# Loading and splitting an MLP's first six weight factors inside the product before it

## The chip, the cores and the metric

The kernel runs on one core of a Trainium2 chip. A core has a matrix engine (TensorE, PE in the profile; its weight loads are shown as PEld), a vector engine (VectorE, DVE), a scalar engine (ScalarE, ACT), a general engine (GpSimd, POOL) and SyncE (SP), which here only issues DMA transfers. Each engine works through its own queue in order and waits on semaphores for the others. The metric is the device time of one execution in microseconds, the median of several executions.

## The reference, cut to what matters

Two layers, each a mixer and a squared-ReLU MLP. The first layer's mixer is an mLSTM, the second's a short gated convolution. Both end in a product with an output matrix of 1024 x 1024, and an MLP follows each.

```python
D_MODEL = 1024; SEQ = 512; DEPTH = 2; D_FF = 4 * D_MODEL

def rms_norm(x, g):
    y = x * lax.rsqrt(jnp.mean(x * x, axis=-1, keepdims=True) + EPS)
    return y * g

def sqrelu_mlp(x, w_up, w_down):
    h = jax.nn.relu(x @ w_up)
    return (h * h) @ w_down

def reference(...):
    for i in range(DEPTH):
        g = norm_g[i]
        h = rms_norm(x, g[0])
        h = mlstm_mixer(h, ...) if i == 0 else short_conv_mixer(h, ...)   # ends: ... @ w_out
        x = x + rms_norm(h, g[1])
        h = sqrelu_mlp(rms_norm(x, g[2]), w_mlp_up[i], w_mlp_down[i])
        x = x + rms_norm(h, g[3])
    return x
```

All is float32.

## The kernel before

**Precision.** Every float32 operand of a product is split into a high factor, which is the operand rounded to the matrix engine's faster format, and a low factor, the rest. `split` (lines 80-85) does it in two instructions: a cast on ScalarE (line 81) and a subtraction on VectorE (line 82). `mm3` (lines 113-118) then issues three matmuls for one product: high by high, high by low, low by high.

**Buffers.** Tiles come from rings of fixed size. The ring `u` has 15 places (`NU`) of 8 KB per partition; a split weight piece or factor takes one, and so does each part of the transposed activations. The ring `raw` has 7 places (`NRAW`) for weights as they land from memory. The ring `t2` has 8 places (`NT2`) of 2 KB for intermediate values. In PSUM, where matmuls write, there are 4 banks `pu`, 2 banks `pd` and 2 banks `pt`.

**The order of instructions.** The code emits instructions in a program order. A planner of the framework, which runs when the program is built, sets the order in each engine's queue from that order and from when it takes each instruction and its buffer to be ready. A ready instruction can so be put ahead of an earlier one that waits. Beside that the code holds a queue of its own: `put_off(us, fn)` (line 141) stores a function, and `step(us)` (line 144), called along the products with their estimated microseconds, calls it when the time is up. It puts off the transposes of a token tile (`turn`, line 274) by `LATE` = 10.4.

**The output product.** `last_product` (lines 297-363) multiplies 4 token tiles of 128 tokens (t = 0 to 3) by a 1024 x 1024 matrix in two halves of 512 columns. Its 8 weight pieces (4 for each half) are loaded and split and stay in 8 places of `u` until the last token tile has used them. The order on PE is: half 0 of t=0 and t=1, half 1 of t=0 and t=1, then both halves of t=2, then both of t=3. `done` (line 320) takes each result out of its `pd` bank with a square-and-sum on ScalarE (line 198) and a multiplication on VectorE (line 332). After the second half of a token tile, `tail` adds the normed row to the residual (line 291), norms it again (line 269) and puts its transposes off (line 278, PE). `Seven.take` (line 228) then splits the transposed tile into the parts that the MLP needs. For t=0 and t=1 these are the parts `a11` and `a12`. For t=2 and t=3 they are `p1`, `r3`, `p4`, `n2` and `a22`, sums and differences of all four blocks. With t=0 it also takes two places of `raw` (`keep`).

**The MLP.** The up product of `mlp` (lines 899-965) is computed in 8 column groups (`quad(g)`, 512 columns each) by a scheme of seven block products in place of eight (class `Quad`, lines 818-894). One block product (`prod`, line 805) is 24 matmuls with a moving size of 256. `begin` (line 842) loads the weight block (0,0), splits it, multiplies it by `a11` and copies the result to a `t2` tile (line 847). `first_done` (line 849) does the same with block (1,0) and `a12`, adding in the same PSUM bank. These two need only token tiles 0 and 1. `run` (line 854) does the other five products, which need `p1`, `r3`, `p4`, `n2` and `a22` and so all token tiles. For the first 3 groups (`AHEAD`), `begin` and `first_done` stand at the head of `mlp`, before any `run`, so that PE has work while the last token tiles are being normed. Then the groups alternate with the down product (`down`, line 921), and `last_product` ends the MLP too, without a mixer after it.

Program order around the change, twice in the kernel (line 803 with line 968, line 1007 with line 1008): the whole of `last_product`, then `mlp` with 3 x `begin`, 3 x `first_done`, `flush()`, `run` of groups 0 and 1, `down(0)` and so on.

Of the kernel before, what the change touches and what calls it, by code (L numbers as in the profile page):

```python
# [36 lines left out]
AHEAD = 3  # L37
# [3 lines left out]
def tile_hybrid_trunk(  # L41
# [29 lines left out]
    def pd():  # L71
        return psum("pd", 2)
# [40 lines left out]
    def mm3(o, lhs, rhs, first, last):  # L113
        lh, ll = lhs
        rh, rl = rhs
        nc.tensor.matmul(o, lh, rh, start=first, stop=False, skip_group_check=True)  # L116
        nc.tensor.matmul(o, lh, rl, start=False, stop=False, skip_group_check=True)  # L117
        nc.tensor.matmul(o, ll, rh, start=False, stop=last, skip_group_check=True)  # L118


    def rows_of(hT, k, t):
        c = (t % 2) * P
        return [hT[k // 2][:, i, t // 2, k % 2, c : c + P] for i in range(2)]
# [20 lines left out]
    def step(us):  # L144
        for item in queue:
            item[0] -= us
        while queue and queue[0][0] <= 0:
            queue.pop(0)[1]()

    def flush(n=0):  # L150
        while len(queue) > n:
            queue.pop(0)[1]()
# [22 lines left out]
    def gain(i, k):  # L175
        g = const.tile([P, D], F32, tag="gain", name="gain", bufs=2)
        nc.gpsimd.dma_start(g, norm_g[i, k].partition_broadcast(P))
        return g
# [79 lines left out]
    def halves(n=2):  # L258
        return [slice(i * D // n, (i + 1) * D // n) for i in range(n)]
# [34 lines left out]
            if store is not None:  # L294
                nc.sync.dma_start(store[:, hs], xt[:, hs])

    def last_product(wm, r0, hT, g, tail, accs=None, ends=False):

        flush()
        ws = {}  # L300
        parts = [halves() for _ in range(NT)]
        if ends:
            parts[NT - 1] = halves()[:1] + halves(4)[2:]
        ygs = [[] for _ in range(NT)]
        mss = [None] * NT

        def ks(o, t, cs, k0, k1):
            hf, c0 = divmod(cs.start, 512)
            n = cs.stop - cs.start
            for k in range(k0, k1):  # L310
                w = ws[hf][k // 2]
                mm3(
                    o[:, 0:n],
                    rows_of(hT, k, t),
                    (w[:, 0, k % 2, c0 : c0 + n], w[:, 1, k % 2, c0 : c0 + n]),
                    k == 0,
                    k == KO - 1,
                )

        def done(o, t, cs):  # L320
            n = cs.stop - cs.start
            step(BLOCK * n / 512)
            i = len(ygs[t])
            if i == 0:
                mss[t] = small(len(parts[t]))
            yg = half_kb(n=n)
            ygs[t].append((cs, yg))
            last = i == len(parts[t]) - 1
            o = o[:, 0:n]
            if accs is None:  # L330
                part_ms(o, mss[t], i)
                nc.vector.tensor_tensor(out=yg, in0=o, in1=g[:, cs], op=ALU.mult)  # L332
            else:
                y = accs[t][:, cs]
                nc.vector.tensor_tensor(out=y, in0=y, in1=o, op=ALU.add)  # L335
                part_ms(y, mss[t], i)
                eng = nc.vector if ends and t == NT - 1 else nc.gpsimd
                eng.tensor_tensor(out=yg, in0=y, in1=g[:, cs], op=ALU.mult)
            if last:
                tail(t, ygs[t], mss[t])  # L340

        for hf in range(2):
            ws[hf] = [
                piece(
                    wm[r0 + 2 * i * P : r0 + 2 * (i + 1) * P, halves()[hf]].rearrange(
                        "(k p) m -> p k m", p=P
                    ),
                    2,
                )
                for i in range(4)  # L350
            ]
            os = [pd() for _ in range(2)]
            first = KO - 2 if hf == 0 else 0
            for t in range(2):
                ks(os[t], t, parts[t][hf], 0, first)
            for t in range(2):
                ks(os[t], t, parts[t][hf], first, KO)
                done(os[t], t, parts[t][hf])
        for t in range(2, NT):
            for cs in parts[t]:  # L360
                o = pd()
                ks(o, t, cs, 0, KO)
                done(o, t, cs)
# [3 lines left out]
    xT = Plain()  # L367
# [174 lines left out]
    a = T1[0:H, :]  # L542
# [203 lines left out]
    hT = [None] * (KO // 2)  # L746
# [41 lines left out]
    def tail_to(gn, nxt, aside=False):  # L788
        def tail(t, yg, ms2):
            if nxt is None:  # L790
                add_normed(yg, ms2, xs[t], out2[t * P : (t + 1) * P, :])
            else:
                add_normed(yg, ms2, xs[t], None)
                pre_norm(t, xs[t], gn, nxt, LATE)
                if aside:
                    nc.gpsimd.dma_start(xd[t], xs[t])

        return tail
# [1 line left out]
    for t in range(NT):  # L800
        load_x(t)
    xT2 = Seven()
    last_product(w_out_mlstm[0], 0, hT, gain(0, 1), tail_to(gain(0, 2), xT2, True))

    def prod(o, fw, fx, first):

# [11 lines left out]
    class Quad:  # L818
# [20 lines left out]
        def values(self):  # L839
            return by_tile(half_kb())  # L840

        def begin(self, a=None):
            f = self.factor(a if a is not None else self.block(0, 0))
            self.x = pu()
            prod(self.x, f, self.xT.f["a11"], True)
            self.s1 = self.values()
            nc.scalar.copy(self.s1, by_tile(self.x))

        def first_done(self, c=None):
            f = self.factor(c if c is not None else self.block(1, 0))  # L850
            prod(self.x, f, self.xT.f["a12"], False)
            self.take(0, 0, self.values(), by_tile(self.x))

# [42 lines left out]
    def by_tile(o):  # L896
        return o.rearrange("p (u n) -> p u n", u=2)

    def mlp(i, xT, gy, tail, ends=False):
        NG = FF // P // G  # L900
        hs = [None] * (FF // P // 2)

        def quad(g):
            def take(nh, half, c, o):
                j = 2 * g + nh
                if o is not None:
                    nc.scalar.activation(c, o, AF.Relu)
                else:
                    o = c
                nc.vector.scalar_tensor_tensor(  # L910
                    out=c, in0=o, scalar=0.0, in1=c, op0=ALU.max, op1=ALU.mult
                )
                if hs[j] is None:
                    hs[j] = pair()
                split(hs[j][:, 0, half], hs[j][:, 1, half], c)

            return Quad(w_up[i], g * 512, g * 512 + 256, xT, take)

        ys = []

        def down(g):
            if g == 0:
                ys.extend(token_tiles())
            for hf, cs in enumerate(halves()):
                ws = [
                    piece(
                        w_dn[i][r * P : (r + 2) * P, cs].rearrange("(k p) m -> p k m", p=P), 2
                    )
                    for r in (g * G, g * G + 2)
                ]  # L930
                for t in range(NT):
                    o = pd()
                    for k in range(G):
                        w = ws[k // 2]
                        mm3(
                            o,
                            rows_of(hs, g * G + k, t),
                            (w[:, 0, k % 2, :], w[:, 1, k % 2, :]),
                            k == 0,
                            k == G - 1,  # L940
                        )
                    yh = ys[t][:, cs]
                    if g == 0:
                        nc.scalar.copy(yh, o)
                    else:
                        nc.vector.tensor_tensor(out=yh, in0=yh, in1=o, op=ALU.add)  # L946


        flush(2)
        quads = [quad(g) for g in range(NG)]  # L950
        for qd in quads[:AHEAD]:
            qd.begin()
        for qd in quads[:AHEAD]:
            qd.first_done()
        flush()
        for g in range(2):
            quads[g].run(True)
        for g in range(NG - 2):
            down(g)
            quads[g + 2].run(g + 2 < AHEAD)  # L960
            if g == NG - 4:
                xs[:] = token_tiles()
                for t in range(NT):
                    nc.gpsimd.dma_start(xs[t], xd[t])  # L964
        last_product(w_dn[i], FF - D, hs[-(KO // 2) :], gy, tail, ys, ends)

    xT3 = Plain()
    mlp(0, xT2, gain(0, 3), tail_to(gain(1, 0), xT3))


    us = {}
    yT = [None] * (KO // 2)
# [31 lines left out]
        [(w_in_conv[0], seg[i % 3] + (i // 3) * P) for i in range(3 * KO)], xT3, take_c, 6  # L1004
    )
    xT4 = Seven()
    last_product(w_out_conv[0], 0, yT, gain(1, 1), tail_to(gain(1, 2), xT4, True))
    mlp(1, xT4, gain(1, 3), tail_to(None, None), ends=True)


# [29 lines left out]
```

## Time and profile before

| | us |
|---|---|
| three runs: median (lowest to highest) | 1138.42 (1138.06 to 1138.58) |
| the profiled execution | 1139.16 |
| its span, from the first to the last instruction | 1137.4 |
| PE busy in the span | 1098.1 |
| DVE busy | 733.9 |
| ACT busy | 450.2 |

The profile shows one execution with start and duration of each instruction, and for each idle stretch of an engine the instruction that ended it ("<-"). Times in its rows are microseconds from the start of the span. A row of grouped instructions gives the line of the code, the engine, the operation, the output and input tiles, the shape and the count. The times of matmul ends are modelled, and a few per cent of matmul records can be missing. The granted clock (PEclk) is the share of full speed that TensorE had in a stretch of time.

### The profile page before, as it was taken

The numbers are of one execution on the slowest core, as the hardware profiler recorded it, in microseconds if no ns is written. First come the engines' busy times: TensorE is split into PE (matmuls) and PEld (weight loads), VectorE is DVE, ScalarE is ACT, GpSimd is POOL, SyncE is SP. The second block draws the span as 40 slices with busy tenths as digits, with TensorE's granted clock in tenths as the row PEclk, the third lists the DMA queues.
The fourth block names the chain that finished last, engine by engine and source line by source line (L and its number), as shares of the span: only waits on it lengthen the run. The fifth ranks groups of instructions, "written<-read, shape, count | busy, mean of one in ns | idle before, by whom it ended". The sixth has DMA issues, their size and how long they took to land.

```text
span 1137.4 us, 15341 instructions
## 1 busy us (share of the span) xinstructions
PE 1098.1 (97%) x6243; PEld 949.2 (83%) x6243; DVE 733.9 (65%) x993; ACT 450.2 (40%) x692; POOL 64.9 (6%) x108
## 2 busy tenths in 40 slices
PE   8999999969999999999999999996999999999997
PEld 5878887869798898899889888786978889889986
DVE  5552665469776776767685444346977677676763
ACT  6431543346444244234363222234644424423421
POOL 2000100110000000000130000011000000000011
PEclk9999999989999999999999999998999999999999
DMA  8420363044353243153535331104435324315301
GB/s 263 135 67 1 101 214 93 38 158 157 117 162 96 71 130 104 64 186 103 138 88 172 113 106 59 56 37 145 151 119 160 94 74 130 104 64 185 103 28 56
DMA packets 112749, 126.35 MB, mean 111 GB/s; under 512 B 4998, under 2 KB 85158, under 8 KB 112679
## 3 DMA queue, kind: packets, MB, share of 16 engines
q1 hardware_dynamic: 109366, 113.31, 32.0%
q0 software_dynamic: 3312, 12.06, 2.9%
q8 instruction: 49, 0.80, 0.3%
q14 instruction: 22, 0.17, 0.1%
HBM read 119.07 MB, written 6.29 MB: 110 GB/s over the span
## 4 chain that ended last, share of the span: by engine, by line
PE 73%; DVE 11%; issue 9%; ACT 3%; DMA 2%; POOL 1%; SPq 0%; POOLq 0%; DVEq 0%; ACTq 0%
PE pu L116 12%; PE pu L117 12%; PE pu L118 12%; PE pd L117 11%; PE pd L118 11%; PE pd L116 11%; DVE u L82 4%; DMA raw<-in_w_in_mlstm_dram 1%; ACT u L81 1%; ACT junk L198 1%; DMA raw<-in_w_mlp_up_dram 1%; DVE t L910 1%; POOL small L190 1%; DVE u L291 1%; DVE hb L82 1%
## 5 line engine op out<-in xcount | busy, mean ns | idle before, releaser
L116 PE MATMUL pu<-u 128*128 128x256 f32 (+1 forms) x1296 | 408.2, 315 | 19.1 <-ACT u L81 18.8
L118 PE MATMUL pu<-u 128*128 128x256 f32 (+1 forms) x1296 | 403.2, 312 | 4.4 <-DVE u L82 4.4
L117 PE MATMUL pu<-u 128*128 128x256 f32 (+1 forms) x1296 | 404.8, 312 | 0.4 <-DVE u L82 0.4
L82 DVE TENSOR_TENSOR u<-raw,u 128x1024 fp32r<-128x1024 f32 (+1 forms) x248 | 295.4, 1204 | 137.7 <-ACT u L81 137.4
L81 ACT CAST u<-raw 128x1024 fp32r<-128x1024 f32 (+1 forms) x248 | 251.4, 1035 | 272.0 <-PE pd L118 118.3
L116 PEld LDWEIGHTS pu<-u 128*128 128x128 f32 x1296 | 246.0, 190 | 36.5 <-ACT u L81 20.5
L118 PEld LDWEIGHTS pu<-u 128*128 128x128 f32 x1296 | 245.1, 189 | 20.7 <-DVE u L82 6.0
L117 PEld LDWEIGHTS pu<-u 128*128 128x128 f32 x1296 | 246.0, 190 | 16.3 <-DVE u L82 1.3
L117 PE MATMUL pd<-u,hb 128*128 128x512 f32 (+1 forms) x648 | 254.2, 392 | 1.3 <-DVE u L82 1.3
L116 PE MATMUL pd<-u,hb 128*128 128x512 f32 (+1 forms) x648 | 254.5, 393 | 0.7 <-ACT u L81 0.4
L118 PE MATMUL pd<-u,hb 128*128 128x512 f32 (+1 forms) x648 | 253.9, 392 | 0.0
L117 PEld LDWEIGHTS pd<-u,hb 128*128 128x128 f32 x648 | 121.7, 188 | 30.1 <-DVE u L82 2.9
L116 PEld LDWEIGHTS pd<-u,hb 128*128 128x128 f32 x648 | 121.5, 188 | 29.3 <-DVE t L332 1.2
L118 PEld LDWEIGHTS pd<-u,hb 128*128 128x128 f32 x648 | 121.7, 188 | 28.1
L81 ACT CAST hb<-t 128x512 fp32r<-128x512 f32 x80 | 49.1, 621 | 86.1 <-DVE t L910 74.2
L946 DVE TENSOR_TENSOR u<-u,pd 128x512 f32<-128x512 f32 x80 | 54.7, 683 | 29.6 <-PE pd L118 29.5
L198 ACT ACTIVATE junk<-u 128x512 bf16<-128x512 f32 (+1 forms) x49 | 30.5, 623 | 77.7 <-DVE u L335 48.3
L82 DVE TENSOR_TENSOR hb<-t,hb 128x512 fp32r<-128x512 f32 x80 | 53.4, 687 | 3.8 <-ACT hb L81 3.6
L332 DVE TENSOR_TENSOR t<-pd,gain 128x512 f32<-128x512 f32 x16 | 11.0, 688 | 36.3 <-ACT junk L198 36.3
L964 POOL DMA_DIRECT2D u<-xd x8 | 4.3, 536 | 493.6 <-PE pu L118 493.6
L910 DVE SCALAR_TENSOR_TENSOR t<-t 128x512 f32<-128x512 f32 x48 | 31.5, 685 | 0.0
L291 DVE SCALAR_TENSOR_TENSOR u<-t,small,u 128x512 f32<-128x512 f32 (+1 forms) x33 | 22.9, 733 | 10.8 <-POOL small L190 10.8
(153 smaller groups left out, 664.8 us busy)
## 6 DMA issues: line engine op xcount, KB each, us to landing
raw<-in_w_mlp_up_dram SPq DMA_DIRECT2D x76, 512.0 KB, 3.7
raw<-in_w_mlp_down_dram SPq DMA_DIRECT2D x64, 512.0 KB, 3.5
raw<-in_w_in_mlstm_dram SPq DMA_DIRECT2D x24, 512.0 KB, 4.8
raw<-in_w_in_conv_dram SPq DMA_DIRECT2D x24, 512.0 KB, 5.3
raw<-in_w_out_mlstm_dram SPq DMA_DIRECT2D x8, 512.0 KB, 4.1
xd<-u POOLq DMA_DIRECT2D x8, 512.0 KB, 2.9
u<-xd POOLq DMA_DIRECT2D x8, 512.0 KB, 5.8
raw<-in_w_out_conv_dram SPq DMA_DIRECT2D x8, 512.0 KB, 3.5
```

Source lines behind the costliest of these rows:

```text
L81: hi = nc.scalar.copy(dst_hi, src)
L82: lo = nc.vector.tensor_tensor(out=dst_lo, in0=src, in1=dst_hi.bitcast(F32), op=ALU.subtract)
L116: nc.tensor.matmul(o, lh, rh, start=first, stop=False, skip_group_check=True)
L117: nc.tensor.matmul(o, lh, rl, start=False, stop=False, skip_group_check=True)
L118: nc.tensor.matmul(o, ll, rh, start=False, stop=last, skip_group_check=True)
L190: nc.gpsimd.tensor_tensor(out=r, in0=r, in1=mhalf[:, 0:1], op=ALU.pow)
L198: nc.scalar.activation(junk(n), src, AF.Square, scale=float(D) ** -0.5, accum_out=ms[:, i : i + 1])
L291: nc.vector.scalar_tensor_tensor(out=xt[:, hs], in0=y, scalar=r, in1=xt[:, hs], op0=ALU.mult, op1=ALU.add)
L332: nc.vector.tensor_tensor(out=yg, in0=o, in1=g[:, cs], op=ALU.mult)
L910: nc.vector.scalar_tensor_tensor(out=c, in0=o, scalar=0.0, in1=c, op0=ALU.max, op1=ALU.mult)
L946: nc.vector.tensor_tensor(out=yh, in0=yh, in1=o, op=ALU.add)
L964: nc.gpsimd.dma_start(xs[t], xd[t])
```

## The change

`mlp` becomes a generator in three parts. The first part makes the eight `Quad` objects and calls a new `prepare` on the first three: load block (0,0) and split it. The second part calls `prepare_more` on them: load block (1,0) and split it. The third part is the rest, with `begin` and `first_done` using the prepared factors. `last_product` takes a function `ahead` and calls it at the head of the token tiles t=2 and t=3, so that the first part is emitted between t=1 and t=2, and the second between t=2 and t=3. The gains that `mlp` needs are made by functions called in its third part. Both MLPs are treated alike. No instruction is added or removed; the order of the program changes.

```diff
-    def last_product(wm, r0, hT, g, tail, accs=None, ends=False):
+    def last_product(wm, r0, hT, g, tail, accs=None, ends=False, ahead=None):
...
         for t in range(2, NT):
+            if ahead is not None:
+                ahead()
             for cs in parts[t]:
                 o = pd()
                 ks(o, t, cs, 0, KO)
...
-    last_product(w_out_mlstm[0], 0, hT, gain(0, 1), tail_to(gain(0, 2), xT2, True))
...
+        def prepare(self):
+            self.f1 = self.factor(self.block(0, 0))
+
+        def prepare_more(self):
+            self.f2 = self.factor(self.block(1, 0))
+
         def begin(self, a=None):
-            f = self.factor(a if a is not None else self.block(0, 0))
+            f = self.factor(a) if a is not None else self.f1
             self.x = pu()
             prod(self.x, f, self.xT.f["a11"], True)
...
         def first_done(self, c=None):
-            f = self.factor(c if c is not None else self.block(1, 0))
+            f = self.factor(c) if c is not None else self.f2
             prod(self.x, f, self.xT.f["a12"], False)
...
-    def mlp(i, xT, gy, tail, ends=False):
+    def mlp(i, xT, gain_of, tail_of, ends=False):
...
+        quads = [quad(g) for g in range(NG)]
+        for qd in quads[:AHEAD]:
+            qd.prepare()
+        yield
+        for qd in quads[:AHEAD]:
+            qd.prepare_more()
+        yield
+        gy, tail = gain_of(), tail_of()
 
         flush(2)
-        quads = [quad(g) for g in range(NG)]
         for qd in quads[:AHEAD]:
             qd.begin()
...
-    mlp(0, xT2, gain(0, 3), tail_to(gain(1, 0), xT3))
+    m = mlp(0, xT2, lambda: gain(0, 3), lambda: tail_to(gain(1, 0), xT3))
+    last_product(
+        w_out_mlstm[0], 0, hT, gain(0, 1), tail_to(gain(0, 2), xT2, True), ahead=lambda: next(m)
+    )
+    for _ in m:
+        pass
...
-    last_product(w_out_conv[0], 0, yT, gain(1, 1), tail_to(gain(1, 2), xT4, True))
-    mlp(1, xT4, gain(1, 3), tail_to(None, None), ends=True)
+    m = mlp(1, xT4, lambda: gain(1, 3), lambda: tail_to(None, None), ends=True)
+    last_product(
+        w_out_conv[0], 0, yT, gain(1, 1), tail_to(gain(1, 2), xT4, True), ahead=lambda: next(m)
+    )
+    for _ in m:
+        pass
```

## The prediction, made before the changed kernel ran

> **What bounds the kernel now.** I read the page's engine totals first, then the costliest groups, then the waits, then the timeline of each engine around the longest PE wait.
>
> ```profile
> span 1137.4 us, 15341 instructions
> PE 1098.1 (97%) x6243; PEld 949.2 (83%) x6243; DVE 733.9 (65%) x993; ACT 450.2 (40%) x692; POOL 64.9 (6%) x108
> ...
> L116 PE MATMUL pu<-u 128*128 128x256 f32 (+1 forms) x1296 | 408.2, 315 | 19.1 <-ACT u L81 18.8
> ```
>
> PE is busy for 1098.1 of 1137.4 us, so 39.3 us of idle time are all that a new order can win besides the clock. Of these, 18.8 us stand before one group, waiting for the cast of a split (line 81). The timeline of PE has them in two places, one for each mixer's output product with the MLP behind it:
>
> ```profile
> 233.79 1.04 PE L278 MATMUL pt<-ident,t 128*128 128x128 f32 x8
> ...
> 243.97 0.58 PE L116 MATMUL pu<-u 128*128 128x256 f32 x1 [9.14 <-ACT u L81]
> ...
> 774.11 1.03 PE L278 MATMUL pt<-ident,t 128*128 128x128 f32 x8
> ...
> 784.29 0.58 PE L116 MATMUL pu<-u 128*128 128x256 f32 x1 [9.15 <-ACT u L81]
> ```
>
> PE ends the transposes of t=2 at 234.8 (775.1) and starts `begin` 9.1 us later. The ScalarE timeline shows why:
>
> ```profile
> 234.86 0.59 ACT L247 COPY t<-pt 128x512 f32<-128x512 f32 x1
> ...
> 237.05 1.14 ACT L81 CAST u<-t 128x512 fp32r<-128x512 f32 x2
> 240.70 0.63 ACT L198 ACTIVATE junk<-u 128x512 bf16<-128x512 f32 x1 [2.51 <-DVE u L291]
> ...
> 241.32 1.12 ACT L81 CAST u<-raw 128x512 fp32r<-128x512 f32 x2
> 242.35 0.61 ACT L81 CAST u<-t 128x512 fp32r<-128x512 f32 x1
> 242.87 4.84 ACT L81 CAST u<-raw 128x1024 fp32r<-128x1024 f32 x5
> ```
>
> The weights' casts (128x1024) come right behind the five casts of t=2's parts (`p1` and `r3` at 237.05, `p4` and `n2` at 241.32, `a22` at 242.35). The input of `a22` was copied at 234.86, and ScalarE idled for 2.51 us before 240.70, yet `a22` waited for `p4` and `n2`. I read this as places of the ring `u` being given out in program order: `a22` and the six factors stand behind `p4`, and `p4` behind the chain on VectorE. The weights were not late:
>
> ```profile
> 185.57 1.50 SPq L828 DMA_DIRECT2D raw<-in_w_mlp_up_dram  x2
> ...
> SPq L828 <- DVE u L82: 92.6, 15, 59.2
> ```
>
> The last two loads before the gap are issued by 187, and the next waits 59.2 us for a place of `raw` that only a split frees.
>
> **What follows the gap** decides how much of it is won. The windows (busy time, instructions, then granted clock, DMA share and GB/s):
>
> ```profile
> 190.00:234.00 44.00, 43.81 (x198) 35.32 (x197) 16.13 (x29) 13.43 (x34) 5.08 (x9) 1.00 0.10 40
> ...
> 244.00:250.00 6.00, 6.00 (x38) 5.74 (x39) 6.00 (x7) 4.12 (x5) 0.58 (x1) 0.74 0.47 132
> 250.00:256.00 6.00, 6.00 (x54) 6.00 (x53) 3.28 (x3) 1.70 (x3) 0.00 (x0) 1.00 1.09 360
> 264.00:300.00 36.00, 32.90 (x252) 30.53 (x250) 33.73 (x44) 16.04 (x22) 0.00 (x0) 1.00 0.47 147
> ...
> 784.00:790.00 6.00, 5.71 (x26) 5.45 (x27) 6.00 (x8) 4.03 (x5) 0.00 (x0) 0.52 0.32 96
> 790.00:796.00 6.00, 6.00 (x53) 6.00 (x52) 3.64 (x4) 2.27 (x4) 0.00 (x0) 1.00 1.02 320
> 804.00:840.00 36.00, 33.58 (x263) 31.85 (x262) 33.73 (x45) 16.09 (x22) 0.00 (x0) 1.00 0.45 144
> ```
>
> Three things are to be seen. In the output product (190 to 234) PE is full while VectorE and ScalarE have 28 and 30 us free. Behind the gap the clock is low for some us: 38 matmuls in 6 us against 54 in the next 6, which is 6 x 16/54 = 1.8 us lost; in the second place 26 against 53, less 0.3 idle, up to 2.7. And from 264 to 300 VectorE is the fuller engine (33.73 of 36 against 32.90), with PE idle for 3.1 us (2.4 in the second place). So the gain goes through two engines, and the later one decides.
>
> **The change part by part.** Moved are 2 x 6 loads, casts and subtractions; none is added or removed. Their price:
>
> ```profile
> L82 DVE TENSOR_TENSOR u<-raw,u 128x1024 fp32r<-128x1024 f32 x240 | 290.1, 1221 | 137.0 <-ACT u L81 136.7
> ...
> L81 ACT CAST u<-raw 128x1024 fp32r<-128x1024 f32 x240 | 246.7, 1049 | 269.4 <-PE pd L118 118.3 <-PE pu L118 71.6 <-DVE raw L860 32.7
> ```
>
> *Where they go.* By count of `u`: at t=2 eight weight pieces and two token tiles hold 10 of 15 places. The first three factors make 13, `a11` and `a12` make 15. The second three need places that the pieces of half 0 free when t=3's half 0 ends (about 228), and one that the old token tiles free earlier. Then 2 + 6 + 1 token tile + 4 pieces make 13, and with t=3 done the five parts make 14: all fit. Three casts are 3.1 us, three subtractions 3.7 us, in an output product with 28 us free: I cost them at nothing. If that cover is gone, an eviction waits, which is a rival below. The loads are earlier on SP's queue, where the output product's own pieces are already through, and the later loads (blocks of `run`) get their `raw` places about 10 us earlier.
>
> *PE.* The gap of 9.1 goes and the cold clock with it: 10.9 us (11.9 in the second place). Three `begin` products take 3 x 24 matmuls, at 54 in 6 us 8.0 us, so PE is at 242.8 and wants `first_done`, which must wait until the copy of `begin`'s result (line 847) has left the bank.
>
> ```profile
> L847 ACT COPY t<-pu 128x512 f32<-128x512 f32 x16 | 9.4, 586 | 23.2 <-PE pu L118 23.2
> ...
> 243.77 1.41 DVE L269 SCALAR_TENSOR_TENSOR t<-u,small,gain 128x512 f32<-128x512 f32 x2
> 245.10 5.76 DVE L82 TENSOR_TENSOR u<-raw,u 128x1024 fp32r<-128x1024 f32 x5
> ...
> 252.79 1.23 DVE L82 TENSOR_TENSOR u<-raw,u 128x1024 fp32r<-128x1024 f32 x1 [1.93 <-ACT u L81]
> 254.81 1.23 DVE L860 TENSOR_TENSOR raw<-raw 128x1024 f32<-128x1024 f32 x1 [0.79 <-DMA raw<-in_w_mlp_up_dram]
> 256.30 1.23 DVE L870 TENSOR_TENSOR raw<-raw 128x1024 f32<-128x1024 f32 x1 [0.26 <-DMA raw<-in_w_mlp_up_dram]
> ```
>
> That copy's `t2` tile comes in program order behind the two tiles of t=3's norm (line 269), written until 245.2. If `t2` is also given out in order, PE waits from 242.8 until 245.2 + 0.6 = 245.8 at worst, 3.0 us; at best nothing. This new wait holds only PE's later products; t=3's transposes stand in it. I take 1.2, nearer to none because line 269 need only have started. PE is then ahead by 9.7 (7.9 to 10.9) when `first_done` ends.
>
> [...]
>
> *VectorE.* Without the six subtractions after 245.10, and with the raw blocks there, its work from line 860 on (254.81) can start at 245.10: 9.7 us earlier. Lines 860 and 870 (2 x 1.22), which need only raw blocks, may go ahead of 245.10 too: up to 12.1.
>
> *Sum.* PE is ahead by 9.7, VectorE by 9.7 to 12.1, and what VectorE has more than PE comes off the 3.1 (2.4) us that PE waits in `run`. I take 10.7 a place, 21.4 in all; the bounds are 7.9 and 12.1 a place. After `run(1)` the down product fills PE, so the shift stays. The profiled execution took 1139.16 (span 1137.4 and 1.76 around it), so 1117.8 by it. The median of the runs lies 0.74 lower, which gives **1117.0**, with 1114.2 to 1122.6 for this case.
>
> **The rivals.**
>
> *Only the first three factors move up in effect.* If the second three get their places only behind `a22`, their casts start at 242.87 as now, just where PE ends `begin`: PE keeps most of its gain, but three subtractions (3.7) stay behind 245.10, and VectorE is ahead by 6.0 to 8.4. At 7.2 a place: 1124.0. For it speaks that the second three need freed places, against it that these come free at about 228.
>
> *The splits hold up an eviction.* The second three come free with the end of t=3's half 0, when its result must leave `pd` too:
>
> ```profile
> 228.46 0.60 ACT L198 ACTIVATE junk<-pd 128x512 bf16<-128x512 f32 x1 [0.79 <-PE pd L118]
> ...
> L332 DVE TENSOR_TENSOR t<-pd,gain 128x512 f32<-128x512 f32 x16 | 11.0, 688 | 36.3 <-ACT junk L198 36.3
> ```
>
> Queued behind three casts are line 198, then line 332, then the bank that PE wants. If t=2's eviction stands behind them, t=3's half 1 is late by 3.1 + 0.8 + 0.7 = 4.6, leaving 6.1 a place: 1126.2. Against it: a result has one half product until its bank is wanted, some eight in the 44 us from 190 to 234, so 5.5 us.
>
> *GpSimd waits for a split.* Two power steps of t=3's norm (line 190) run on GpSimd. If each waits a whole subtraction (1.22), t=3 is 2.4 late and 8.3 a place is left: 1121.8. [...] The trace speaks against its deciding here:
>
> ```profile
> L190 POOL TENSOR_TENSOR small<-small,mhalf 128x1 f32<-128x1 f32 x32 | 18.7, 584 | 164.7 <-DVE small L185 154.7 <-DVE small L189 9.8
> ```
>
> 584 ns is the mean of 32, with little room for waits of 1.2 us.
>
> *VectorE runs further ahead* and PE's waits in `run` vanish: 10.9 + 3.1 and 11.9 + 2.4, 28.3 in all: 1110.1.
>
> *Slower: the `raw` ring turns out of phase.* The blocks (0,0) and (0,1) of `run(0)` now land during the output product and hold two of seven places until `run(0)` has used them, some 40 us later, and every later load takes its place in a new order. In the 12 pairs of `down` and `run` that follow in the two MLPs, a piece of `w_down` may then stand behind a block still in use, and PE waits for one load:
>
> ```profile
> raw<-in_w_mlp_up_dram SPq DMA_DIRECT2D x76, 512.0 KB, 3.7
> raw<-in_w_mlp_down_dram SPq DMA_DIRECT2D x64, 512.0 KB, 3.5
> ```
>
> At 3.6 us a pair this costs 43 and gives 1160. It decides from 21.4/12 = 1.8 us a pair. Against it: PE is nearly full in those pairs now, and a shift that is alike for all loads changes no phase.
>
> *The change does nothing:* the planner leaves the splits where they are because their places come no earlier. 1138.4. Against it is the count of `u`.
>
> **How the numbers follow.** Forecast 0.62; first three only 0.11; GpSimd 0.04; eviction 0.05; VectorE further ahead 0.09; ring out of phase 0.05; nothing 0.04. The range 1111 to 1126.5 takes in the bounds of the forecast, the three smaller gains and most of the larger one. Faster by over 0.2% (2.3 us, about what a measurement here can tell from no change): 0.91; within: 0.04; slower: 0.05.
>
> **What would show it.** Right: six 128x1024 casts on ScalarE between 188 and 233 and none from 234 to 245; no PE idle over 3 us at the head of either MLP; granted clock 1.00 there; line 860 before or at 245; PE nearly full through 190 to 234 as now. Wrong: an idle stretch of PE behind three `begin` products (line 847 or a cast as releaser); idle PE within the output product; or the gain at the head lost again in `run` to VectorE's subtractions, then PE waits there would grow above 3.1 us. The least sure step is the sum of VectorE's and PE's lead: whichever is smaller decides, and both were read from an order that the planner will draw anew.

## The result, and the profile after

The changed kernel takes **1112.45 us** (median of four runs, 1112.23 to 1112.79), against 1138.28 (1138.06 to 1138.58) for the kernel before beside it. The ratio is **0.9773, with a 95% interval of 0.9756 to 0.9790**: 25.8 us are gone. The forecast was 1117.0, a gain of 21.4; the time lies within the range, 1111 to 1126.5, but below the forecast case's own 1114.2 to 1122.6. The profiled execution took 1112.23 with a span of 1110.5. Every median in this document is one of fast runs; one slow run, of e2 (2194.31 us), is left out of it.

The page of the changed kernel, its totals and two groups:

```profile
span 1110.5 us, 15339 instructions
PE 1091.1 (98%) x6243; PEld 944.9 (85%) x6243; DVE 733.0 (66%) x993; ACT 450.4 (41%) x692; POOL 65.7 (6%) x108
...
L116 PE MATMUL pu<-u 128*128 128x256 f32 (+1 forms) x1296 | 405.6, 313 | 0.5 <-ACT u L81 0.5
...
L190 POOL TENSOR_TENSOR small<-small,mhalf 128x1 f32<-128x1 f32 x32 | 20.5, 641 | 161.0 <-DVE small L185 151.0
```

The idle 19.1 us in front of the L116 group are down to 0.5. VectorE's and ScalarE's busy times are those of before to within 0.9 us: work was moved, none removed. PE's idle time in the span fell from 39.3 to 19.4 us, 19.9 less, and its busy time by 7.0. So over a quarter of the gain came out of time that the page had counted as *busy*.

The ScalarE timeline, columns as before (start, duration, engine, line, operation, tiles, count, idle time before it and what ended it):

```profile
185.45 1.05 ACT L81 CAST u<-raw 128x1024 fp32r<-128x1024 f32 x1 [0.79 <-PE pu L117]
186.89 1.04 ACT L81 CAST u<-raw 128x1024 fp32r<-128x1024 f32 x1
...
188.87 1.05 ACT L81 CAST u<-raw 128x1024 fp32r<-128x1024 f32 x1
...
218.83 1.05 ACT L81 CAST u<-raw 128x1024 fp32r<-128x1024 f32 x1
...
223.63 1.05 ACT L81 CAST u<-raw 128x1024 fp32r<-128x1024 f32 x1 [0.17 <-PE pd L118]
225.54 1.06 ACT L81 CAST u<-raw 128x1024 fp32r<-128x1024 f32 x1
...
233.44 0.60 ACT L198 ACTIVATE junk<-pd 128x512 bf16<-128x512 f32 x1 [4.55 <-PE pd L118]
...
242.28 1.99 ACT L81 CAST u<-raw 128x1024 fp32r<-128x1024 f32 x2
244.17 1.55 ACT L854 COPY t<-pu 128x512 f32<-128x512 f32 x3
```

The six factors are cast at the head of the output product and within it: three at 185 to 190, when the places of `u` are free, and three at 218.8 to 226.6, one by one. Between t=3's last eviction (L198 at 233.44) and 242.28 there is no weight cast; the two at 242.28 are `run(0)`'s own. The copies of `begin`'s results (L847 before, L854 now) come behind all of them.

PE at the same place:

```profile
233.19 1.04 PE L278 MATMUL pt<-ident,t 128*128 128x128 f32 x8
233.98 0.37 PE L116 MATMUL pu<-u 128*128 128x256 f32 x1
...
244.07 1.01 PE L278 MATMUL pt<-ident,t 128*128 128x128 f32 x6 [1.53 <-DVE t L269]
```

`begin` starts at 233.98 in place of 243.97, right behind the transposes of t=2. A new wait of 1.53 us stands behind the three `begin` products, as the prediction had it. The instruction that waits is the transposes of t=3, whose input line 269 writes. `first_done` could have filled the time, but the copies it needs (L854) start only at 244.17; e5 below tests why.

VectorE:

```profile
228.38 1.22 DVE L867 TENSOR_TENSOR raw<-raw 128x1024 f32<-128x1024 f32 x1
...
231.99 1.22 DVE L877 TENSOR_TENSOR raw<-raw 128x1024 f32<-128x1024 f32 x1
...
244.50 3.49 DVE L82 TENSOR_TENSOR u<-raw,u 128x1024 fp32r<-128x1024 f32 x3
247.91 0.68 DVE L248 TENSOR_TENSOR t<-pt,t 128x512 f32<-128x512 f32 x1
```

And the same last row in the kernel before:

```profile
260.96 0.68 DVE L248 TENSOR_TENSOR t<-pt,t 128x512 f32<-128x512 f32 x1
```

Both sums of `run(0)` (L860 and L870 before, L867 and L877 now) have moved into the output product as well. The first of t=3's parts (L248) is formed 13.05 us earlier.

To measure the head of an MLP I take a stretch that every version has: from t=3's last eviction (L198 on `pd`) to the first copy of a `down(0)` result on ScalarE. I call it a **place**; there are two. The work in it is not always quite the same: 21 matmuls of `down(0)` stand ahead of that copy here, but 24 and 14 in e2's two places and 14 in e11's. One of these starts 0.23 us after the other, so seven are worth 1.6 us. The windows of the kernel before (each row: window, length, then busy us and count of PE, PEld, DVE, ACT, POOL, then granted clock, DMA share, GB/s):

```profile
234.04:302.10 68.06, 55.24 (x421) 52.10 (x419) 60.79 (x77) 35.68 (x53) 2.79 (x5) 0.92 0.49 156
774.37:842.73 68.36, 56.13 (x421) 53.20 (x419) 60.85 (x77) 35.71 (x54) 2.22 (x4) 0.93 0.46 147
```

Of the changed kernel, with the output product ahead of it:

```profile
189.40:233.40 44.00, 43.81 (x198) 35.33 (x197) 24.78 (x38) 16.71 (x38) 5.99 (x9) 1.00 0.35 112
...
233.44:288.68 55.24, 52.30 (x421) 50.32 (x419) 51.43 (x69) 30.10 (x47) 2.79 (x5) 1.00 0.42 135
761.39:816.64 55.25, 52.41 (x421) 50.43 (x419) 51.42 (x69) 30.14 (x47) 2.22 (x4) 1.00 0.41 125
```

The places are 12.82 and 13.11 us shorter, 25.9 together, which is the whole gain of the medians (the two spans differ by 26.9; 0.6 of that lies ahead of the first place). The stretch between them kept its length (472.27 before, 472.71 after), and so about did the rest behind them (294.7, 293.9). The output product is as full as before, 43.81 of 44 us, though VectorE now has 24.78 us of work in it (16.13 before).

### The profile page after: what moved, and what is told of

It reads as the page before. It is cut to its first block, busy times and chain, and to the rows that moved or that the text cites. A ratio compares the mean times of both kernels' runs of the same rounds, so it can differ in the third digit from the quotient of the medians.

```text
span 1110.5 us, 15339 instructions
## 1 busy us (share of the span) xinstructions
PE 1091.1 (98%) x6243; PEld 944.9 (85%) x6243; DVE 733.0 (66%) x993; ACT 450.4 (41%) x692; POOL 65.7 (6%) x108
## 4 chain that ended last, share of the span: by engine, by line
PE 85%; DVE 8%; issue 3%; ACT 2%; DMA 1%; POOL 1%; SPq 0%; POOLq 0%; DVEq 0%; ACTq 0%
PE pu L116 14%; PE pu L118 14%; PE pu L117 14%; PE pd L117 13%; PE pd L118 13%; PE pd L116 13%; DVE u L82 3%; PE pt L278 1%; ACT u L81 1%; DMA raw<-in_w_in_mlstm_dram 1%; DVE u L291 1%; PE pt L683 1%; PE pd L697 1%; POOL small L190 0%; DVE t L918 0%
## 5 line engine op out<-in xcount | busy, mean ns | idle before, releaser
L116 PE MATMUL pu<-u 128*128 128x256 f32 (+1 forms) x1296 | 405.6, 313 | 0.5 <-ACT u L81 0.5
L116 PEld LDWEIGHTS pu<-u 128*128 128x128 f32 x1296 | 244.5, 189 | 16.4 <-ACT u L81 0.9
L116 PE MATMUL pd<-u,hb 128*128 128x512 f32 (+1 forms) x648 | 254.5, 393 | 0.7 <-ACT u L81 0.4
L116 PEld LDWEIGHTS pd<-u,hb 128*128 128x128 f32 x648 | 121.6, 188 | 28.7 <-DVE t L332 1.2
L198 ACT ACTIVATE junk<-u 128x512 bf16<-128x512 f32 (+1 forms) x49 | 30.5, 623 | 75.5 <-DVE u L335 48.2
L190 POOL TENSOR_TENSOR small<-small,mhalf 128x1 f32<-128x1 f32 x32 | 20.5, 641 | 161.0 <-DVE small L185 151.0
L335 DVE TENSOR_TENSOR u<-u,pd 128x512 f32<-128x512 f32 (+1 forms) x17 | 11.1, 655 | 27.7 <-PE pd L118 27.7
```

The costliest lines, as they stand in the source:

```text
L190: nc.gpsimd.tensor_tensor(out=r, in0=r, in1=mhalf[:, 0:1], op=ALU.pow)
L198: nc.scalar.activation(junk(n), src, AF.Square, scale=float(D) ** -0.5, accum_out=ms[:, i : i + 1])
```

## The experiments

All times are medians beside runs of the kernel before on the same chip; lengths of places are read as above from each one's own profile. For e2 that is the fastest of three runs, 1126.74; the others took 1130.04 and 1130.38.

| | us | ratio to before (95%) | places, us | DVE busy in them | PE idle in them |
|---|---|---|---|---|---|
| changed kernel | 1112.45 | 0.9773 (0.9756–0.9790) | 55.24, 55.25 | 51.43, 51.42 | 2.94, 2.84 |
| e1 first three alone | 1124.69 | 0.9882 (0.9865–0.9898) | 61.82, 60.86 | 56.07, 55.99 | 6.32, 6.34 |
| e2 second three alone | 1130.04 | 0.9921 (0.9904–0.9938) | 63.79, 61.27 | 58.52, 58.61 | 9.14, 9.14 |
| e3 loads alone | 1137.65 | 0.9999 (0.9990–1.0009) | 68.07, 67.74 | – | – |
| e6 first MLP alone | 1124.54 | 0.9882 (0.9867–0.9897) | 55.22, 67.90 | 51.42, 60.84 | 2.82, 11.68 |
| e4 before, PE filled | 1146.71 | 1.0077 (1.0065–1.0090) | 73.29, 69.11 | 61.40, 61.28 | 8.39, 6.77 |
| e5 own place for a copy | 1117.88 | 0.9827 (0.9813–0.9840) | 57.40, 57.36 | 51.45, 51.42 | 3.84, 3.82 |
| e5 three places | 1117.41 | 0.9820 (0.9807–0.9834) | 57.38, 57.39 | – | – |
| e7 sums held back | 1122.26 | 0.9862 (0.9847–0.9877) | 60.00, 60.10 | 53.95, 53.97 | 6.39, 6.16 |
| e8 order | 1112.83 | 0.9777 (0.9764–0.9791) | 55.23, 55.20 | 51.41, 51.41 | 2.85, 2.80 |
| e9 own place, order | 1114.54 | 0.9792 (0.9779–0.9805) | 56.18, 56.17 | 51.42, 51.41 | 2.96, 2.88 |
| e10 sums, order | 1119.28 | 0.9833 (0.9820–0.9847) | 58.75, 58.91 | 53.89, 53.96 | 5.32, 5.17 |
| e11 two sums out | 1105.13 | 0.9708 (0.9695–0.9722) | 49.85, 50.00 | 46.75, 46.90 | 0.00, 0.03 |

### Which part of the change does it

**e1: the first three factors alone.** The second three are loaded and split in `first_done`, as before.

```diff
         def first_done(self, c=None):
-            f = self.factor(c) if c is not None else self.f2
+            f = self.factor(c if c is not None else self.block(1, 0))
...
             qd.prepare()
         yield
-        for qd in quads[:AHEAD]:
-            qd.prepare_more()
         yield
```

> Only the first three factors are loaded and split ahead; the second three stand in first_done as before. Theory (two leads, VectorE's decides): PE starts begin right behind the transposes of t=2, but three subtractions (3.7 us) stay behind t=3's norm, so 9 to 9.5 of the 13 us a place are kept: 1119 to 1121 us. Rival (only the start of PE counts): 1112 to 1114 us. The prediction's own sum for this case was 1124.0.

Measured 1124.69: a miss, with less gain than the theory of that moment gave, and the 1124.0 of the prediction's rival nearly to the point. The gap is gone, but PE waits later:

```profile
255.82 0.58 PE L118 MATMUL pu<-u 128*128 128x256 f32 x1 [3.78 <-DVE u L82]
```

VectorE still has three weight subtractions and one sum more to do in the place (56.07 us of work in place of 51.43) and PE runs into them. The windows show what such a wait costs beside its own length:

```profile
255.80:257.00 1.20, 1.18 (x5) 1.18 (x6) 1.20 (x2) 0.00 (x0) 0.00 (x0) 0.50 0.90 292
...
260.00:261.00 1.00, 1.00 (x7) 1.00 (x6) 1.00 (x2) 0.68 (x2) 0.00 (x0) 0.50 0.02 5
261.00:262.00 1.00, 1.00 (x10) 1.00 (x10) 1.00 (x2) 1.00 (x2) 0.00 (x0) 0.92 0.00 0
```

The clock stays at 0.50 from the end of the wait to about 261.2, 5.4 us, with 6 or 7 matmuls in a window of 1 us in place of 10.

**e2: the second three alone.** `begin` loads and splits its own factor as before.

```diff
         def begin(self, a=None):
-            f = self.factor(a) if a is not None else self.f1
+            f = self.factor(a if a is not None else self.block(0, 0))
...
-        for qd in quads[:AHEAD]:
-            qd.prepare()
         yield
```

> Only the second three factors are split ahead; the first three stand in begin as before. Theory (two leads): PE idles some 9 us before begin as in the kernel before, but VectorE has three subtractions less behind the gap and may be 2 to 4 us a place ahead: 1130 to 1135 us. Rival (only the start of PE counts): no gain, 1137 to 1139 us.

Measured 1130.04, at the lower end of what was expected. The gap of 9.14 us is untouched, yet in the profiled run the places are 4.3 and 7.1 us shorter (5.0 and 5.5 with the same number of `down(0)` matmuls), since behind the gap PE waits for nothing:

```profile
250.00:290.00 40.00, 40.00 (x342) 40.00 (x341) 38.47 (x46) 22.40 (x32) 0.00 (x0) 1.00 0.52 164
```

The same window of the kernel before:

```profile
250.00:290.00 40.00, 37.64 (x311) 36.47 (x309) 35.87 (x44) 21.64 (x32) 0.00 (x0) 1.00 0.53 169
```

It has 31 records less, about 3.6 us of PE at 40 us for 342, but shows only 2.36 us of idle time. I read the other 1.2 us as waits of matmuls for their operand that the records count as busy.

**e3: the loads alone**, with cast and subtraction left where they were.

```diff
         def prepare(self):
-            self.f1 = self.factor(self.block(0, 0))
+            self.r1 = self.block(0, 0)
...
         def begin(self, a=None):
-            f = self.factor(a) if a is not None else self.f1
+            f = self.factor(a if a is not None else self.r1)
```

(and `prepare_more` and `first_done` likewise)

> All six blocks are loaded ahead, none is split ahead: the splits stand in begin and first_done as before. Theory (the places of the split factors in program order were late, not the loads): 1136 to 1140 us, PE idle 9 us at both places. Rival (earlier loads bring the gain): 1112 to 1120 us.

Measured 1137.65, ratio 0.9999: nothing. The weights were not late; the splits were. Whether a split waited for its place in `u` or only for its turn in the order was read from the timeline; no run gives the factors a ring of their own.

**e6: the first MLP alone.**

```diff
-    m = mlp(1, xT4, lambda: gain(1, 3), lambda: tail_to(None, None), ends=True)
-    last_product(
-        w_out_conv[0], 0, yT, gain(1, 1), tail_to(gain(1, 2), xT4, True), ahead=lambda: next(m)
-    )
-    for _ in m:
+    last_product(w_out_conv[0], 0, yT, gain(1, 1), tail_to(gain(1, 2), xT4, True))
+    for _ in mlp(1, xT4, lambda: gain(1, 3), lambda: tail_to(None, None), ends=True):
         pass
```

> Only the first MLP's six factors are prepared ahead; the second MLP is as before. Theory (the gain is made at each place by itself): half, 1125 to 1126 us. Rival (part of it comes from a new order elsewhere in the program): more than 1.5 us away from 1125.4.

Measured 1124.54, 0.5 under the expected range: half the gain, one place at 55.22 and the other at 67.90. Each place is a gain by itself, and nothing is given back further on.

### Is it the clock?

**e4: the kernel before, with PE kept busy over the gap** by 72 extra matmuls whose result is not used.

```diff
         quads = [quad(g) for g in range(NG)]
+        warm, f = pu(), xT.f["a11"]
+        for _ in range(72):
+            nc.tensor.matmul(
+                warm[:, 0:256], f[:, 0, 0, 0:P], f[:, 0, 1, :], start=True, stop=True
+            )
         for qd in quads[:AHEAD]:
```

> The kernel before, with 72 matmuls of 128x256 into a bank that nobody reads put in PE's idle stretch before begin (72 x 0.117 us = 8.4 us): the clock stays up, the wait for the splits stays. If the clock is worth what the window counts gave and PE's lead decides: 1.5 to 2.7 us a place, 1133 to 1135.5 us. If VectorE's lead decides (it waits for loads and is late in run): 0 to 1 us a place, 1136.5 to 1138.5 us.

Measured 1146.71: slower than before, a miss. The gap is filled, but the planner drew a new order behind it and PE waits twice for VectorE:

```profile
268.22 0.39 PE L118 MATMUL pu<-u 128*128 128x256 f32 x1 [3.29 <-DVE u L82]
...
286.89 0.58 PE L118 MATMUL pu<-u 128*128 128x256 f32 x1 [3.48 <-DVE u L82]
```

Behind both the clock is at 0.50 (rows in the last section), so the run doesn't isolate the clock's share. It shows only that filling the gap in this way wins nothing while the splits stay where they are.

### Which engine decides

In the changed kernel both leads are there: PE's (gap and cold clock gone, less the new wait) and VectorE's. Two edits act on one of them each.

**e5: take PE's new wait away.** Group 0's copy of `begin`'s result gets a ring of its own, so that it no longer stands behind t=3's norm in `t2` (which has 7 places then).

```diff
-NT2 = 8
+NT2 = 7
...
-            self.s1 = self.values()
+            if self.cols[0] == 0:
+                self.s1 = by_tile(big.tile([P, 512], F32, tag="s1", name="s1", bufs=1))
+            else:
+                self.s1 = self.values()
```

> The changed kernel, with a ring of one place for the copy of begin's result of group 0, and 7 in place of 8 places in t2 (the same memory): the copy need not stand behind t=3's norm. Theory: PE's new idle stretch of 1.5 us behind the third begin goes. If PE's lead decides, 1.5 us a place, 1109.5 us; if VectorE's decides, 0 to 0.5 a place, 1111.5 to 1112.5 us. A smaller t2 ring may cost something elsewhere, then above 1112.5 us.

Measured 1117.88, 5 us *slower* than the changed kernel: a miss for both theories. The copy now comes 6 us earlier, ahead of line 269:

```profile
238.06 0.58 ACT L857 COPY s<-pu 128x512 f32<-128x512 f32 x1
```

The wait of 1.53 us is gone, so the reading of it was right: the copy's place in `t2` stood behind line 269. But PE got nothing for it. The second form, a ring of three places for all three copies (`bufs=3`, `NT2 = 5`), does the same:

> As the one before, with a ring of three places for the copies of all groups and 5 places in t2. Theory: as the one before for the idle stretch; a ring of 5 for the other values may hold up run and the convolution: anything from 1109.5 us to 1120 us.

1117.41. What became later is on VectorE. In the changed kernel three of four weight subtractions are done ahead of `run(0)`'s values (L892 to L895), and the fourth right behind the first value:

```profile
262.92 3.49 DVE L82 TENSOR_TENSOR u<-raw,u 128x1024 fp32r<-128x1024 f32 x3
266.33 0.68 DVE L892 TENSOR_TENSOR t<-pu,t 128x512 f32<-128x512 f32 x1
266.93 1.21 DVE L82 TENSOR_TENSOR u<-raw,u 128x1024 fp32r<-128x1024 f32 x1
```

In e5_own_place, where the last of these values is L897, two come behind them:

```profile
266.18 1.21 DVE L82 TENSOR_TENSOR u<-raw,u 128x1024 fp32r<-128x1024 f32 x1
...
268.52 0.68 DVE L897 TENSOR_TENSOR t<-pu,t 128x512 f32<-128x512 f32 x1
...
272.73 1.22 DVE L82 TENSOR_TENSOR u<-raw,u 128x1024 fp32r<-128x1024 f32 x1
273.86 0.68 DVE L82 TENSOR_TENSOR hb<-s,hb 128x512 fp32r<-128x512 f32 x1
274.47 1.22 DVE L82 TENSOR_TENSOR u<-raw,u 128x1024 fp32r<-128x1024 f32 x1
```

and PE waits for the first of these:

```profile
274.00 0.39 PE L118 MATMUL pu<-u 128*128 128x256 f32 x1 [1.55 <-DVE u L82]
```

**e7: hold VectorE back.** The two sums of `run(0)` are ordered behind t=3's norm in place of going ahead into the output product.

```diff
-            tt(out=a, in0=a, in1=b, op=ALU.add)
+            held = self.cols[0] == 0
+            with tc.issue_after(normed_last[0]) if held else ExitStack():
+                tt(out=a, in0=a, in1=b, op=ALU.add)
...
-            tt(out=b, in0=b, in1=d, op=ALU.add)
+            with tc.issue_after(normed_last[0]) if held else ExitStack():
+                tt(out=b, in0=b, in1=d, op=ALU.add)
```

(`normed_last[0]` is t=3's last line 269)

> The changed kernel, with the two sums of weight blocks of run(0) (lines 867 and 877 of the changed kernel, 2 x 1.22 us) queued on VectorE behind t=3's norm, in place of being done during the output product. If VectorE's lead decides: up to 2.4 us a place lost, 1115 to 1117.5 us. If PE's lead decides: under 0.5 a place, 1112 to 1113.5 us.

Measured 1122.26: 9.8 us slower than the changed kernel, 4.8 a place. The direction is that of the theory, the size is double. VectorE's busy time in a place grew by the 2.5 us; the rest may come from the order again, since run(1)'s subtractions stand behind `run(0)`'s values here too.

**e8, e9, e10: the order held fixed.** To part the order from the engines, the blocks, sums and splits of `run(1)` are emitted within `run(0)`, ahead of its values.

```diff
-            d = self.block(1, 1)
-            tt(out=b, in0=b, in1=d, op=ALU.add)
-            w = self.factor(b)
...
             prod(y, w6, f["n2"], False)
+            if then is not None:
+                then.ready = then.prep()
...
-            quads[g].run(True)
+            quads[g].run(True, quads[1] if g == 0 else None)
```

(`prep` returns the blocks and the two factors; `run` uses them where they are ready)

> The changed kernel, with run(1)'s weight blocks, sums and first splits emitted within run(0), ahead of run(0)'s values. VectorE's order at that place is already about this one in the changed kernel, so if only VectorE's order and its busy time count, the time is that of the changed kernel: 1111.0 to 1113.0. If the emitted order also draws the later pairs of run and down anew, it can go either way by more than 2 us.

> e5_own_place with the same order emitted. Theory: that kernel lost 2.15 us a place only because run(1)'s splits had come behind run(0)'s values on VectorE; with them ahead the loss goes, and the 1.5 us wait of PE stays away: 1109.5 to 1112.5. Rival: the loss has another cause in the ring of intermediate tiles: 1116.5 to 1118.5.

> e7_sums_held with the same order emitted. Theory: of the 4.8 us a place, 2.4 are the two sums' own time on VectorE behind t=3's norm and the rest is run(1)'s splits behind run(0)'s values; with these ahead 2.4 a place remain: 1116.0 to 1118.0. Rival: the sums' delay alone does it all: 1121 to 1123.

Measured 1112.83, 1114.54 and 1119.28. e8 has the changed kernel's order and its time. With the order fixed, e9 is 3.3 us faster than e5_own_place and e10 3.0 faster than e7: 1.2 and 1.2 us a place were the order alone. The windows of e9 and then e10, first place:

```profile
233.59:289.77 56.18, 53.22 (x421) 50.66 (x419) 51.42 (x69) 29.98 (x47) 2.79 (x5) 1.00 0.41 133
```

```profile
233.54:292.29 58.75, 53.43 (x421) 50.63 (x419) 53.89 (x71) 29.77 (x47) 2.79 (x5) 1.00 0.39 127
```

e9 missed its 1109.5 to 1112.5. PE's 1.53 us wait is gone there, and PE idles for 2.96 us all the same (2.94 in the changed kernel): the wait only moved. So PE's own lead doesn't decide. The place is even 0.95 longer than e8's; whether the smaller `t2` ring costs that is not tested. In e10 VectorE's 2.46 us more work makes the place 3.5 us longer than e8's (expected 2.4, so the time is above the 1116 to 1118 forecast): all of it, and 1.1 us more.

**e11: take VectorE work away.** One more direction was open: if VectorE decides, less work there must shorten the place. e9 without the sum `a + d` in the first two groups:

```diff
-            tt(out=a, in0=a, in1=d, op=ALU.add)
+            if self.cols[0] >= 1024:
+                tt(out=a, in0=a, in1=d, op=ALU.add)
```

> e9_own_place_order without one block sum (128x1024, 1.22 us on VectorE) in each of run(0) and run(1), in both MLPs, so that the n2 product of these groups works on other weights; matmuls, casts and loads are all there. Theory: VectorE decides the place, so the two sums' 2.4 us come off it, as far as the 3 us that PE idles there allow: 51.42 us of VectorE becomes 49.0, the place 53.5 to 54.2 in place of 56.18, the time 1109.5 to 1111.0. Rival: PE's own lead decides, the place stays at 56 and the time at 1113.5 to 1115.

Measured 1105.13, 9.4 us under e9: 4.7 a place for two instructions of 1.22 us. The window of its first place:

```profile
233.77:283.62 49.85, 49.85 (x414) 48.98 (x412) 46.75 (x64) 29.10 (x47) 2.80 (x5) 1.00 0.48 152
```

PE has no idle time left at all. The theory's direction held, its limit didn't: I had expected at most the 3 us that PE showed as idle. The place fell by 6.3, but 1.6 of this are the seven matmuls of `down(0)` that stand behind its end here, and about as much came back further on. Over equal work the gain is 4.7 a place. Of this 2.96 were PE's idle time, and 1.7 had counted as busy (53.22 against 49.85 and the 1.6).

Why two sums are worth twice their time is shown only in part. They are 2.4 us of VectorE's work, and its waits for casts on ScalarE (line 81) fell from 3.1 to 1.5 us in the place, which leaves 0.7 of the 4.7 open. Besides, a sum is a link of the chain that leads to a factor (sum, cast, subtraction), so e11 takes out a link along with the time. No run here parts the two.

## Why the prediction was right, and where its size was off

**Where the splits go: right.** The six casts stand ahead of the gap, though earlier than said (the first at 185.45 against 188, the second three from 218.8 against 228). All three of the second start before t=3's half 0 ends at 228, so they didn't wait for its last piece. The two casts at 242.28, in a stretch where the prediction wanted none, are `run(0)`'s own. PE stayed as full there as before. That cost nothing, as forecast. e3 shows that the casts and subtractions, not the loads, had been late.

**PE's 9.1 us: right.** The gap is gone in both places.

**The cold clock: right.** Forecast were 1.8 and up to 2.7 us. Behind the two gaps of the kernel before the granted clock was 0.50 for 3.06 and 5.43 us:

```profile
243.97:247.03 3.06, 3.06 (x13) 2.80 (x14) 3.06 (x4) 3.06 (x4) 0.58 (x1) 0.50 0.07 24
784.29:789.72 5.43, 5.43 (x24) 5.17 (x25) 5.43 (x6) 3.73 (x4) 0.00 (x0) 0.50 0.32 95
```

By the granted clock half of it is lost, 1.5 and 2.7 us; in the changed kernel the clock is 1.00 in the windows of both places. But PE's busy time for the same 421 matmul records fell by more, 2.94 (55.24 to 52.30) and 3.72 (56.13 to 52.41). The granted clock doesn't account for the other 1.4 and 1.0 us. I take them for waits for operands that the records count as busy, as in e2's window.

**The new wait: right.** 1.2 was taken, 1.53 and 1.43 came, with the place in `t2` as its cause (e5). An idle stretch behind `begin` was also named as a sign of being wrong; it was a term of the prediction's own sum, and at its size it is no such sign. The lower bound of 7.9 a place took a wait of 3.0 us and no loss to the clock with it; no run shows that such a wait leaves the clock up. What they show: behind the 1.53 us the clock stayed at 1.00, and behind e4's 3.29 and e1's 3.78 it was 0.50; in the kernel before it fell 2.0 us after PE went idle at the first gap and 4.4 us after at the second (rows in the last section).

**VectorE's lead: at its upper bound.** The upper bound of 12.1 had lines 860 and 870 go ahead of 245.10. They did. Counted from t=3's last eviction, the first of its parts comes at 247.91 - 233.44 = 14.47 in place of 260.96 - 234.04 = 26.92: 12.45 earlier.

**The sum: this is the step that failed in size.** The prediction put PE ahead by 9.7 and VectorE by 9.7 to 12.1 and took 10.7 between them. The places went by 12.82 and 13.11. The first, with its terms read from the windows and waits:

| term, first place | forecast | measured |
|---|---|---|
| gap | 9.1 | 9.14 |
| cold clock | 1.8 | 1.53 |
| new wait | -1.2 | -1.53 |
| PE's waits in `run` and the start of `down(0)`: as idle time | 1.0 | 2.27 |
| the same, counted as busy | 0 | 1.41 |
| sum | 10.7 | 12.82 |

(2.27 is the fall in idle time, 12.82 - 2.94 = 9.88, less 9.14, plus 1.53; 1.41 is the fall in busy time, 2.94, less the clock's 1.53.) The mis-sized term is PE's waits: forecast 1.0, measured 3.7, and 2.7 in the second place. The prediction took a value between the two leads and saw only the 3.1 and 2.4 us of waits that show as idle. But PE's lead and VectorE's are not to be averaged: PE follows VectorE. Take PE's wait away, and the idle time comes back elsewhere (e9); put two sums more on VectorE's path, and the place grows by all of it (e10); take two sums away, and PE has no idle time left (e11). So the place came forward by VectorE's 12.45 and a little more. Had the sum gone by VectorE's upper bound alone, 12.1 a place, it would have given 1114.2. That the time lies within the range in spite of this is in part the range's width.

**The rivals.** *Only the first three*: it didn't happen, but e1 built it and measured 1124.69 against the 1124.0 worked out. *VectorE runs further ahead*: the nearest of all (1110.1, 2.3 us off, against 4.6 for the forecast); PE's waits shrank as it says, though they didn't vanish. *GpSimd waits for a split*: its power step was longer once at a place, 1.46 and 1.47 us, beside a sum (L867) and on t=2's norm (below); those of t=3's norm took 0.55 and 0.56 us. The transposes of t=2 still stand right behind the output product, so nothing was delayed there. *An eviction held up*: no, 43.81 of 44 us. *The `raw` ring out of phase*: no, the stretch between the places is 0.4 us longer in all. *Nothing*: no.

## What to carry to other kernels

When one engine prepares operands for another, work out the lead of each. Here the feeder's decided, and removing a wait of the fed engine alone won nothing (e9). Here the idle time of the matmul engine understated its waits: e11's place without gaps, 51.5 us with the seven matmuls added, is what 55.24 and 68.06 are to be measured against, and not the page's 97% busy. And where instructions get their buffers or their turn in program order, emission order is a resource: what must be ready early has to be emitted early. An edit of a ring or of the emission can draw the order of the other engines anew, which was worth 1 to 2 us a place here.

## What the runs showed of the hardware

**Behind five waits of 3.29 us and more the clock was at 0.50.** Behind e4's waits of 3.29 and 3.48 us and e1's of 3.78 whole microseconds run at 0.50, and so do the stretches behind the gaps of 9.14 and 9.15 us of the kernel before; I read a value between 0.50 and 1.00 as the mean of a window in which the clock changed. Windows of e4, behind its two waits:

```profile
269.20:270.20 1.00, 1.00 (x7) 1.00 (x7) 1.00 (x2) 0.00 (x0) 0.00 (x0) 0.50 0.88 251
...
289.00:290.00 1.00, 1.00 (x6) 1.00 (x6) 1.00 (x2) 0.00 (x0) 0.00 (x0) 0.50 0.26 31
...
292.00:293.00 1.00, 1.00 (x8) 1.00 (x8) 1.00 (x1) 0.59 (x1) 0.00 (x0) 0.71 0.82 207
```

The busy stretch at 0.50 was not the same each time: 3.4 us behind e4's first wait, 5.7 behind its second, 5.4 in e1, 3.1 and 5.4 behind the two gaps of the kernel before. In e1, half of 5.4 us is lost by the granted clock on top of a wait of 3.78; a matmul starts every 0.21 us there and every 0.12 us ahead of the wait, which makes it 2.4 us. So this wait cost over 6 us.

Nor is the time from idle to the lower clock the same. In the kernel before PE is idle from 234.83 and from 775.14; the clock falls at 236.8 and at 779.5, 2.0 and 4.4 us later:

```profile
234.86:236.80 1.94, 0.00 (x0) 0.00 (x0) 1.28 (x3) 0.96 (x2) 0.55 (x1) 1.00 0.00 0
237.00:238.00 1.00, 0.00 (x0) 0.00 (x0) 1.00 (x2) 1.00 (x4) 0.00 (x0) 0.50 0.00 0
...
779.00:779.40 0.40, 0.00 (x0) 0.00 (x0) 0.40 (x2) 0.00 (x0) 0.34 (x1) 1.00 0.00 0
779.60:780.00 0.40, 0.00 (x0) 0.00 (x0) 0.40 (x2) 0.00 (x0) 0.00 (x0) 0.50 0.00 0
```

At e4's first wait it fell only at 268.7, 3.8 us after PE had gone idle and half a microsecond after it had started again: the window from 264.9 to 268.2 shows 1.00, and from 268.68 to 272.08 the matmuls start 0.19 to 0.22 us apart in place of 0.12.

**A power step on GpSimd took 1.46 us beside a sum on VectorE.** In the changed kernel's timeline of GpSimd, the power step of t=2's norm:

```profile
228.56 1.46 POOL L190 TENSOR_TENSOR small<-small,mhalf 128x1 f32<-128x1 f32 x1 [0.42 <-DVE small L185]
```

It has one element per partition, and the group's mean was 584 ns in the kernel before. Here it took 1.46 us, beside the sum L867 that runs on VectorE from 228.38 for 1.22 us; it ends 0.42 us after the sum does. In the second place it took 1.47 us beside the same sum; the group's median is 552 ns, and its mean rose to 641 ns. That the sum held the step up is my reading of these two rows.
